# Feature sums queued behind the delta-rule branch's last evacuation, and accumulating transfers regrouped, in a hybrid transformer block

## The chip, the core and the metric

The kernel runs on one core of a Trainium2 chip. The metric is the device time of one execution in microseconds. A run of a kernel gives the median of several executions; one execution more is taken with the hardware profiler, and all rows shown come from that one.

## What is computed

One block on a sequence of 512 tokens with 1024 features. A projection `w_in` feeds two branches: A, a gated delta rule with 8 heads, and B, retention with 4 heads. Both are gated, added, projected and normed; a feed-forward part with 4096 hidden features follows.

```python
xn = rmsnorm(x, n_mix_pre)
proj = xn @ w_in
qa, ka, va, za, beta_logit, a_dt, qb, kb, vb, gb, gate_a, gate_b = _split_cols(proj, IN_SIZES)
...
oa = chunk_gated_delta_rule(qa, ka, va, beta, g)
oa = rmsnorm(oa, norm_a) * jax.nn.silu(za.reshape(b, s, A_HEADS, A_DV))
ya = oa.reshape(b, s, A_V) @ w_br_a
...
ob = chunk_retention(qb, kb, vb)
ob = rmsnorm(ob, norm_b.reshape(B_HEADS, B_DV)) * jax.nn.silu(gb.reshape(b, s, B_HEADS, B_DV))
yb = ob.reshape(b, s, B_V) @ w_br_b
mix = (jax.nn.sigmoid(gate_a) * ya + jax.nn.sigmoid(gate_b) * yb) @ w_out
x = x + rmsnorm(mix, n_mix_post)
hn = rmsnorm(x, n_mlp_pre)
ff = jnp.square(jax.nn.relu(hn @ w_up)) @ w_down
return x + rmsnorm(ff, n_mlp_post)
```

## The kernel before

**Matmuls.** Every large product is done in three matmuls (`mm3`, L79): both operands are split in a high and a low part, and high x high, high x low and low x high are added in PSUM. `weights` (L86) loads 512 KB of weights from DRAM into a tile `raw` (a DMA on SP), ACT casts it to `whi` (L109) and DVE subtracts to get `wlo` (L110). There are two `raw` buffers and three of `whi` and `wlo`; so SP issues a load when the `wlo` two loads earlier is done, and ACT casts when PE has finished the load three earlier. One load feeds 24 matmuls of 128x512. Products gather in four PSUM banks `mm`; scores and small products use three banks `dl`.

**Branch A.** Its heads go in four pairs `g2`. Each has `recurrence` (a chain of small matmuls with casts `vn` on ACT between them), `values_queries` of the next pair, `gated`, and `ya_partial`, which multiplies the gated rows `og` of a pair by `w_br_a`, in two halves, and adds the four banks of each half into `acc` on DVE (L443). The last, `ya_partial(3, prev)`, runs in head 0 of branch B.

**Branch B.** Each of its four heads computes `scores(h)`: q and k products, `rotary` on DVE (tiles `ro`, then `qr` and `kr` as high and low parts), then the score matmuls `dl<-qr,kr`, masked on DVE with the tile `dec` (one buffer, filled by a POOL DMA). Head 0 then has `ya_partial(3)` and the product for gate A (its four banks are emptied by a `tanh` on ACT, `g_t`, L927); the other heads multiply the head before by `w_br_b`. Last in each head is `outputs`: values and gates, scores times values (`dl<-vr,s`, emptied by DVE's `o` and ACT's `osq`), norm and gating, and transposes of `o`.

Values and gates are computed with fewer products, Strassen-Winograd style, on 2x2 blocks. That needs sums of blocks of the weights and of the activations. The weight sums of head h, `vg_sums[h]`, are made in DRAM: plain copies on SP, trickled behind weight loads, then eight transfers on POOL that add 512 KB each into a copy (L134). They form chains, in the order (2,0), (1,0), (3,0), (2,2), (1,2), (3,2), (0,0), (0,2) of block and part: block 1 adds block 2, block 3 adds block 1; the rest add from `w_in`. They are read by head h's `raw<-sums` loads. The activation sums are `feature_sums` (L745): eight additions into `full` and four pairs of a cast on ACT and a subtraction on DVE into `xsum`, each on 128x1024; they are first read in head 0's `outputs`.

**What sets the order.** The program is written without engine queues; a scheduler sorts the instructions of each engine by priority (written order, with raised priority for weights) and each engine then runs its list strictly in that order. `tc.issue_after(ins)` puts the instructions of a block behind `ins` on its engine; `keep_in_program_order` keeps them in written order. The groups of additions are hung on POOL instructions: a marker of branch A (`pool_marks`) and the `decay` DMA of a head.

Of the kernel before, what the change touches and what calls it, by code (L numbers as in the profile page):

```python
# [15 lines left out]
ALU = mybir.AluOpType  # L16
# [44 lines left out]
def hybrid_block_kernel(ctx: ExitStack, tc: tile.TileContext, a: dict, out: bass.AP):  # L61
    nc = tc.nc
# [53 lines left out]
    class BlockSums:  # L116
# [10 lines left out]
        def copy(self, i, k):  # L127
            nc.sync.dma_start(self.t[i][:, k : k + 2, :], self.first[i][:, k : k + 2, :])

        def add(self):  # L130

            for i, k in ((2, 0), (1, 0), (3, 0), (2, 2), (1, 2), (3, 2), (0, 0), (0, 2)):
                src = (self.w12, self.t[2], self.w12, self.t[1])[i]
                add = nc.gpsimd.dma_start(self.t[i][:, k : k + 2, :], src[:, k : k + 2, :], accum_op=ALU.add)  # L134
                tc.keep_in_program_order(add)

        def weights(self, i, ks):
            return block_weights(self.t[i - 1][:, 2 * ks : 2 * ks + 2, :])
# [235 lines left out]
    def gated_features(o_t, norms):  # L374
        og = [act.tile([P, 4, T], F32R, tag="og", name="og") for _ in range(2)]
        for f in range(4):
            ps = psx.tile([P, 4, P], F32, tag="tr", name="tr", bufs=1)
            for t in range(4):
                transpose(ps[:, t, :], o_t.feature(t, f))
            split_from(ps.rearrange("p t c -> p (t c)"), og[0][:, f, :], og[1][:, f, :], norms(f))  # L380
        return og

    def branch_partial(w, og, krow0):
        for half in range(2):
            yield half, feature_major(w, og, half * 512, 512, 4, krow0)
# [50 lines left out]
    def ya_partial(g2, og):  # L436
        for half, pss in branch_partial(w_br[0], og, 4 * g2):
            for f in range(4):
                dst = acc[:, half * 4 + f, :]
                if g2 == 0:  # L440
                    nc.scalar.copy(dst, pss[f])
                else:
                    nc.vector.tensor_tensor(dst, dst, pss[f], ALU.add)  # L443

    with tc.tile_pool(name="pa", bufs=1) as pa:
        kf = pa.tile([P, 8, T], F32, name="kf")
# [81 lines left out]
        pool_marks = []  # L528
# [167 lines left out]
        def gated(g2, rows, pool):  # L696
            pss = token_major(w_in, x_tile, OFF_ZA + g2 * 512, 8)
            zz = pool.tile([P, 4, T], F32, tag="zz", name="zz")
            gate_rows(pss, rows, lambda t: zz[:, t, :])

        vg_sums = [BlockSums(w_in, OFF_VB + h * 512, OFF_GB + h * 512, f"vg{h}") for h in range(4)]
        with tc.tile_pool(name="pa2", bufs=1) as pa2:
            keys(0, pa2)
            scr = base_inverse(0, pa2)
            vq = values_queries(0, pa2)
            keys(1, pa2)
            double_blocks(pa2, scr, 0)
            og = None
            for g2 in range(4):
                rows = recurrence(g2, vq, pa2)  # L710
                if g2 == 0:
                    double_blocks(pa2, scr, 8)
                    scr = base_inverse(1, pa2)
                if g2 < 3:
                    vq = values_queries(g2 + 1, pa2)
                if g2 == 1:
                    double_blocks(pa2, scr, 16)
                    double_blocks(pa2, scr, 24)
                if g2 in (1, 2):
                    with tc.issue_after(pool_marks[-1].ins):  # L720
                        vg_sums[g2 - 1].add()
                gated(g2, rows, pa2)
                if g2:
                    ya_partial(g2 - 1, og)
                og = gated_features(rows, lambda f: na[:, f % 2 : f % 2 + 1])
        prev = og


    with tc.tile_pool(name="pb", bufs=1) as pb_:
# [6 lines left out]
        def tmp(name):  # L736
            return pb_.tile([P, T], F32, tag="tm", name=name, bufs=8)


        def quarter(kh, th):  # L740
            return [x[:, 4 * kh : 4 * kh + 4, 256 * th : 256 * th + 256] for x in xs]
# [3 lines left out]
        def feature_sums():  # L745
            full = [pb_.tile([P, 2, 4, 256], F32, tag=f"vr{i}", name="full") for i in range(2)]
            a11, a12, a21, a22 = full[0][:, 0], full[0][:, 1], full[1][:, 0], full[1][:, 1]
            for a, (kh, th) in ((a21, (0, 1)), (a22, (1, 1)), (a11, (0, 0)), (a12, (1, 0))):
                h, l = quarter(kh, th)
                nc.vector.tensor_tensor(a, h, l, ALU.add)  # L750
            nc.vector.tensor_tensor(a22, a21, a22, ALU.subtract)
            nc.vector.tensor_tensor(a21, a11, a21, ALU.subtract)
            nc.vector.tensor_tensor(a11, a22, a11, ALU.subtract)
            nc.vector.tensor_tensor(a12, a12, a11, ALU.add)
            for i, a in enumerate((a22, a11, a21, a12)):
                s = pb_.tile([P, 2, 4, 256], F32R, tag=f"xs{i}", name="xsum")
                nc.scalar.copy(s[:, 0], a)
                nc.vector.tensor_tensor(s[:, 1], a, s[:, 0], ALU.subtract)
                quarters[f"s{i + 1}"] = [s[:, 0], s[:, 1]]
# [83 lines left out]
        def scores(h):  # L843
            dec = pb_.tile([P, T], F32, tag="dec", name="dec")
            decay = nc.gpsimd.dma_start(dec, a["c_decay"][h])
            if h in (1, 2):
                with tc.issue_after(decay.ins):
                    vg_sums[h + 1].add()
            qs, ks = (pb_.tile([P, 2, 2, T], F32R, tag=nm, name=nm) for nm in ("qr", "kr"))
            qs, ks = [qs[:, 0], qs[:, 1]], [ks[:, 0], ks[:, 1]]  # L850
            rotary(feature_major(w_in, xs, OFF_QB + h * 256, 256, 8), qs)
            rotary(feature_major(w_in, xs, OFF_KB + h * 256, 256, 8), ks)
            scs = []
            for i in range(4):
                t0 = min(i * P, 256)
                n = T - t0
                ps = psx.tile([P, T], F32, tag="dl", name="dl", bufs=3)
                for kk in range(2):
                    mm3(
                        ps[:, :n],  # L860
                        [ks[j][:, kk, i * P : (i + 1) * P] for j in range(2)],
                        [qs[j][:, kk, t0:T] for j in range(2)],
                        kk == 0,
                        kk == 1,
                    )
                n2 = T - i * P
                sc = tmp("sc")
                nc.vector.tensor_tensor(sc[:, :n2], ps[:, n - n2 : n], dec[:, :n2], ALU.mult)
                sh, sl = (pb_.tile([P, n2], F32R, tag=f"s{i}{j}", name="s") for j in range(2))
                nc.scalar.copy(sh, sc[:, :n2])  # L870
                nc.vector.tensor_tensor(sl, sc[:, :n2], sh, ALU.subtract)
                scs.append((sh, sl))
            return scs
# [44 lines left out]
        for h in range(4):  # L918
            scs = scores(h)
            if h == 0:  # L920
                feature_sums()
                ya_partial(3, prev)
                for half in range(2):
                    pss = gate_product(OFF_GA, half)
                    for f in range(4):
                        ta = tmp("g_t")
                        nc.scalar.activation(ta, pss[f], AF.Tanh, scale=0.5)  # L927
                        dst = acc[:, half * 4 + f, :]
                        nc.vector.scalar_tensor_tensor(dst, ta, 1.0, dst, ALU.add, ALU.mult)
                    nc.gpsimd.dma_start(ya_d[:, half * 4 : half * 4 + 4, :], acc[:, half * 4 : half * 4 + 4, :])  # L930
            else:
                for half, pss in branch_partial(w_br[1], prev, 4 * (h - 1)):
                    for f in range(4):
                        dst = accb[:, half * 4 + f, :]
                        if h == 1:
                            nc.scalar.copy(dst, pss[f])
                        else:
                            nc.vector.tensor_tensor(dst, dst, pss[f], ALU.add)
            if h == 0:
                raw_pools.append((pb_, "ych"))  # L940
            rows = outputs(h, scs)
            prev = gated_features(rows, lambda f: nb[:, 4 * h + f : 4 * h + f + 1])
# [6 lines left out]
        for half in range(2):  # L949
            pss = gate_product(OFF_GBR, half)  # L950
# [22 lines left out]
    with tc.tile_pool(name="pm", bufs=1) as pm:  # L973
# [113 lines left out]
        for grp in range(4):  # L1087
# [8 lines left out]
            for half in range(2):  # L1096
                c0 = grp * 1024 + half * 512
                for tt in [slice(0, 256), slice(256, 512)] if grp + half == 0 else [slice(0, T)]:
                    pss = feature_major(w_up, [h[:, :, tt] for h in hn], c0, 512, 8)
# [6 lines left out]
            if grp < 3:  # L1106
                for half in range(2):
                    pss = token_major(w_down, ff_tile, half * 512, 8, grp * 8)
                    for t in range(4):
                        dst = facc[:, t, half * 512 : half * 512 + 512]  # L1110
# [4 lines left out]
            else:  # L1115
                wk = og_keeps() + ff_keeps()
                for i in range(2):
                    h = pm.tile([P, 8, T], F32R, tag=f"hn{i}", name="keep").rearrange("p k t -> p (k t)")
# [39 lines left out]
```

## Time and profile before

| | us |
|---|---|
| median of 3 runs | 1403.16 |
| lowest and highest | 1402.61 and 1406.29 |
| the profiled execution | 1403.7 |
| its span, first to last instruction | 1402.0 |

| stage, from the span's start | us |
|---|---|
| the two groups of added transfers in branch A | 287.8 to 329.3 and 394.2 to 432.2 |
| head 0: feature sums on DVE | 499.0 to 533.1 |
| head 0: first product that reads them | 601.9 |
| groups behind the `dec` of heads 1 and 2 | 528.8 to 562.1 and 670.2 to 709.4 |

A row of a timeline has the start in us, the duration in us, engine, line, operation, tiles (written <- read), shape and count, and in square brackets how long the engine stood idle before and for what. A row of the waits has the waiting engine and instruction, what it waited for, us in total, times, and the longest. A row of a table of stretches has the stretch, its length, busy us (and instructions) of PE, PEld, DVE, ACT and POOL, the granted PE clock as a share, the share of the DMA engines' time and GB/s. A row of DMA issues has the tiles, the queue, the count, the size and the median us from issue to landing.

### The profile page before, as it was taken

How to read it: one execution, taken by the hardware profiler on the slowest of the kernel's cores; microseconds unless marked ns; L12 is line 12 of the kernel's file. 1: busy time of each engine (PE TensorE's matmuls, PEld its weight loads, DVE VectorE, ACT ScalarE, POOL GpSimd, SP SyncE). 2: the span in 40 equal slices, each digit the busy share in tenths (PEclk: the TensorE clock that was granted, in tenths of full speed). 3: DMA queues.
4: the chain of work that ended last, by engine and by line, in shares of the span. 5: the costliest groups of instructions: out<-in, count | busy, mean ns of one | idle time of the engine just before them, and what ended most of it. 6: DMA issues, size and time to landing. Idle time of an engine off the chain costs nothing.

```text
span 1402.0 us, 17608 instructions
## 1 busy us (share of the span) xinstructions
PE 1373.8 (98%) x6670; PEld 1125.1 (80%) x6670; DVE 869.2 (62%) x1539; ACT 613.4 (44%) x1134; POOL 86.4 (6%) x136
## 2 busy tenths in 40 slices
PE   8999999999999998999999999999999999999997
PEld 6888787787888877887878878878788888888886
DVE  5599889853765584367467576575685334344445
ACT  6778564725534241353543343443454333232331
POOL 1112300211011002000100000000000000000000
PEclk9999999999999999999999999999999999999999
DMA  5244624377365337672782442541724322323321
GB/s 158 76 136 139 191 76 151 116 159 205 104 130 115 103 128 158 175 220 83 176 224 61 142 138 89 187 143 62 252 80 134 100 95 95 101 91 104 105 76 61
DMA packets 88311, 180.08 MB, mean 128 GB/s; under 512 B 6079, under 2 KB 19537, under 8 KB 87714
## 3 DMA queue, kind: packets, MB, share of 16 engines
q1 hardware_dynamic: 77264, 148.39, 33.6%
q0 software_dynamic: 10240, 29.32, 10.5%
q8 instruction: 52, 0.85, 0.2%
q10 hardware_dynamic: 722, 1.25, 0.2%
q14 instruction: 33, 0.27, 0.1%
HBM read 173.17 MB, written 39.32 MB: 152 GB/s over the span
## 4 chain that ended last, share of the span: by engine, by line
PE 55%; DVE 3%; DMA 2%; ACT 1%; issue 1%; DVEq 0%; ACTq 0%; SPq 0%
PE mm L82 14%; PE mm L84 14%; PE mm L83 14%; PE mm L772 9%; PE dl L772 1%; PE dl L82 1%; PE dl L84 1%; PE dl L83 1%; DMA raw<-in_w_in_dram 1%; PE tr L219 1%; DMA raw<-in_w_out_dram 1%; DVE wlo L110 1%; ACT whi L109 0%; DVE tb L966 0%; DVE actT L968 0%
## 5 line engine op out<-in xcount | busy, mean ns | idle before, releaser
L110 DVE TENSOR_TENSOR wlo<-raw,whi 128x1024 fp32r<-128x1024 f32 x232 | 283.4, 1222 | 349.6 <-ACT whi L109 348.5
L109 ACT CAST whi<-raw 128x1024 fp32r<-128x1024 f32 x232 | 243.9, 1052 | 467.9 <-PE mm L83 257.0
L84 PE MATMUL mm<-actT,wlo 128*128 128x512 f32 (+1 forms) x528 | 208.8, 396 | 0.0
L83 PE MATMUL mm<-actT,whi 128*128 128x512 f32 (+1 forms) x528 | 207.4, 393 | 1.2 <-DVE actT L253 1.2
L82 PE MATMUL mm<-actT,whi 128*128 128x512 f32 (+1 forms) x528 | 207.0, 393 | 0.8 <-ACT actT L252 0.8
L82 PEld LDWEIGHTS mm<-actT,whi 128*128 128x128 f32 x528 | 100.0, 190 | 20.9 <-ACT actT L252 1.2
L83 PEld LDWEIGHTS mm<-actT,whi 128*128 128x128 f32 x528 | 100.0, 189 | 20.6 <-DVE actT L253 1.4
L84 PEld LDWEIGHTS mm<-actT,wlo 128*128 128x128 f32 x528 | 100.2, 190 | 18.8
L82 PE MATMUL mm<-hn,whi 128*128 128x512 f32 (+1 forms) x288 | 105.6, 367 | 0.6 <-DVE r L1081 0.5
L82 PE MATMUL mm<-og,whi 128*128 128x512 f32 x256 | 101.1, 395 | 4.6 <-DVE acc L443 4.4
L83 PE MATMUL mm<-hn,whi 128*128 128x512 f32 (+1 forms) x288 | 105.3, 366 | 0.0
L84 PE MATMUL mm<-hn,wlo 128*128 128x512 f32 (+1 forms) x288 | 105.1, 366 | 0.0
L83 PE MATMUL mm<-og,whi 128*128 128x512 f32 x256 | 100.7, 393 | 0.0
L84 PE MATMUL mm<-og,wlo 128*128 128x512 f32 x256 | 100.6, 393 | 0.0
L82 PE MATMUL mm<-whi,actT 128*128 128x512 f32 x216 | 86.2, 399 | 0.0
L83 PE MATMUL mm<-wlo,actT 128*128 128x512 f32 x216 | 85.9, 398 | 0.0
L84 PE MATMUL mm<-whi,actT 128*128 128x512 f32 x216 | 85.6, 397 | 0.0
L772 PE MATMUL mm<-whi,xsum 128*128 128x512 f32 x256 | 80.2, 390 | 0.0
L407 DVE SCALAR_TENSOR_TENSOR c_y<-c_raw,convw,c_y 128x512 f32<-128x512 f32 x96 | 70.5, 751 | 3.4 <-ACT c_y L405 2.8
L82 PEld LDWEIGHTS mm<-hn,whi 128*128 128x128 f32 x288 | 54.3, 188 | 10.2 <-DVE r L1081 0.8
L84 PEld LDWEIGHTS mm<-hn,wlo 128*128 128x128 f32 x288 | 54.2, 189 | 8.8
L83 PEld LDWEIGHTS mm<-hn,whi 128*128 128x128 f32 x288 | 54.3, 188 | 8.6
(319 smaller groups left out, 2463.8 us busy)
## 6 DMA issues: line engine op xcount, KB each, us to landing
raw<-in_w_in_dram SPq DMA_DIRECT2D x105, 512.0 KB, 3.8
raw<-in_w_up_dram SPq DMA_DIRECT2D x36, 512.0 KB, 3.8
sums<-in_w_in_dram SPq DMA_DIRECT2D x32, 512.0 KB, 5.2
raw<-sums SPq DMA_DIRECT2D x32, 512.0 KB, 4.4
raw<-in_w_down_dram SPq DMA_DIRECT2D x32, 512.0 KB, 3.7
raw<-in_w_br_a_dram SPq DMA_DIRECT2D x16, 512.0 KB, 3.9
sums<-in_w_in_dram POOLq DMA_DIRECT2D x16, 512.0 KB, 11.6
sums<-sums POOLq DMA_DIRECT2D x16, 512.0 KB, 7.5
```

The source lines that it names most:

```text
L82: nc.tensor.matmul(ps, lh, rh, start=first, stop=False)
L83: nc.tensor.matmul(ps, lh, rl, start=False, stop=False)
L84: nc.tensor.matmul(ps, ll, rh, start=False, stop=last)
L109: nc.scalar.copy(hi[:, :n], raw[:, :n])
L110: nc.vector.tensor_tensor(lo[:, :n], raw[:, :n], hi[:, :n], ALU.subtract)
L219: nc.tensor.transpose(ps, src, ident)
L407: nc.vector.scalar_tensor_tensor(y, raw[:, j : j + T], tap(j), y, ALU.mult, ALU.add)
L772: m = nc.tensor.matmul(pss[t], lhs[i // 2], rhs[i % 2], start=first and k + i == 0, stop=k + i == 5, skip_group_check=not first,)
```

## The change

Two things are changed. The feature sums of head 0 are written after `ya_partial(3)` and put behind its last `acc` addition on DVE. And the 32 accumulating transfers, unchanged in themselves and in their order, form one sequence from which groups are drawn: 10 and 12 at the two places in branch A and 8 and 2 behind the `dec` of heads 1 and 2, where before each place issued the eight of one head. The lines of the changed kernel are shifted by up to 7; the order on SP stays as it was.

```diff
-        def add(self):
+        def adds(self):
             for i, k in ((2, 0), (1, 0), (3, 0), (2, 2), (1, 2), (3, 2), (0, 0), (0, 2)):
                 src = (self.w12, self.t[2], self.w12, self.t[1])[i]
-                add = nc.gpsimd.dma_start(self.t[i][:, k : k + 2, :], src[:, k : k + 2, :], accum_op=ALU.add)
-                tc.keep_in_program_order(add)
+                yield self.t[i][:, k : k + 2, :], src[:, k : k + 2, :]
...
-                    nc.vector.tensor_tensor(dst, dst, pss[f], ALU.add)
+                    added = nc.vector.tensor_tensor(dst, dst, pss[f], ALU.add)
+        return added if g2 else None
...
+        adds = itertools.chain.from_iterable(sums.adds() for sums in vg_sums)
+        def add_blocks(mark, n):
+            with tc.issue_after(mark.ins):
+                for dst, src in itertools.islice(adds, n):
+                    tc.keep_in_program_order(nc.gpsimd.dma_start(dst, src, accum_op=ALU.add))
...
                 if g2 in (1, 2):
-                    with tc.issue_after(pool_marks[-1].ins):
-                        vg_sums[g2 - 1].add()
+                    add_blocks(pool_marks[-1], 8 + 2 * g2)
...
             if h in (1, 2):
-                with tc.issue_after(decay.ins):
-                    vg_sums[h + 1].add()
+                add_blocks(decay, 8 if h == 1 else 2)
...
             if h == 0:
-                feature_sums()
-                ya_partial(3, prev)
+                with tc.issue_after(ya_partial(3, prev).ins):
+                    feature_sums()
```

On DVE, in head 0 of branch B, from the last rotary step of k to the gate product (`kr`, `sc` and `s` belong to the scores, `acc` to `ya_partial(3)`), the order before ends so:

```order
L753 TENSOR_TENSOR full<-full 128x1024
L868 TENSOR_TENSOR sc<-dl,dec 128x512
L868 TENSOR_TENSOR sc<-dl,dec 128x384
L868 TENSOR_TENSOR sc<-dl,dec 128x256
L754 TENSOR_TENSOR full<-full 128x1024
...
L758 TENSOR_TENSOR xsum<-full,xsum 128x1024 x2
L110 TENSOR_TENSOR wlo<-raw,whi 128x1024
L758 TENSOR_TENSOR xsum<-full,xsum 128x1024
L443 TENSOR_TENSOR acc<-acc,mm 128x512 x4
L110 TENSOR_TENSOR wlo<-raw,whi 128x1024
L443 TENSOR_TENSOR acc<-acc,mm 128x512 x4
```

In the changed kernel the same place reads:

```order
L442 TENSOR_TENSOR acc<-acc,mm 128x512 x4
L110 TENSOR_TENSOR wlo<-raw,whi 128x1024 x2
L442 TENSOR_TENSOR acc<-acc,mm 128x512 x4
L757 TENSOR_TENSOR full<-actT 128x1024
L110 TENSOR_TENSOR wlo<-raw,whi 128x1024
L757 TENSOR_TENSOR full<-actT 128x1024 x3
L110 TENSOR_TENSOR wlo<-raw,whi 128x1024
L758 TENSOR_TENSOR full<-full 128x1024
L759 TENSOR_TENSOR full<-full 128x1024
L765 TENSOR_TENSOR xsum<-full,xsum 128x1024
L760 TENSOR_TENSOR full<-full 128x1024
L110 TENSOR_TENSOR wlo<-raw,whi 128x1024
```

All twelve instructions of the sums, which began among the rotary steps before, now stand behind both sets of `acc` additions, among the `wlo` of the gate product.

On POOL, from the second group in branch A to the first `dec` of branch B (`at` is the marker's tile, `rope` the table that the rotary steps read), the order before is:

```order
L608 AFFINE_SELECT at<-at 128x1024
L134 DMA sums<-in_w_in_dram 128x2x512
L134 DMA sums<-sums 128x1024 x2
L134 DMA sums<-in_w_in_dram 128x2x512
L134 DMA sums<-sums 128x1024 x2
L134 DMA sums<-in_w_in_dram 128x2x512 x2
L731 DMA rope<-in_c_rope_dram 128x1024
```

And in the changed kernel:

```order
L608 AFFINE_SELECT at<-at 128x1024
L708 DMA sums<-sums 128x1024
L708 DMA sums<-in_w_in_dram 128x2x512
L708 DMA sums<-sums 128x1024 x2
L708 DMA sums<-in_w_in_dram 128x2x512 x3
L708 DMA sums<-sums 128x1024 x2
L708 DMA sums<-in_w_in_dram 128x2x512
L708 DMA sums<-sums 128x1024 x2
L738 DMA rope<-in_c_rope_dram 128x1024
```

Twelve additions stand ahead of `rope` in place of eight; three that wait for no sum stand together in the middle, after the end of one head's chain.

Further down POOL's list, from the stores of `ya_d` to its reload behind the heads, the order before is:

```order
L930 DMA ya_d<-acc 128x2048 x2
L845 DMA dec<-in_c_decay_dram 128x512
L134 DMA sums<-in_w_in_dram 128x2x512
L134 DMA sums<-sums 128x1024 x2
L134 DMA sums<-in_w_in_dram 128x2x512
L134 DMA sums<-sums 128x1024 x2
L134 DMA sums<-in_w_in_dram 128x2x512 x2
L845 DMA dec<-in_c_decay_dram 128x512
```

And in the changed kernel:

```order
L936 DMA ya_d<-acc 128x2048 x2
L852 DMA dec<-in_c_decay_dram 128x512
L708 DMA sums<-in_w_in_dram 128x2x512 x2
L852 DMA dec<-in_c_decay_dram 128x512
```

The first `dec` here is head 2's, issued while head 1 runs; two additions follow it where there were eight.

## The prediction

> **What bounds the kernel now.** The page comes first, for the engine that sets the time, then the waits of that engine over the whole run.
>
> ```profile
> PE 1373.8 (98%) x6670; PEld 1125.1 (80%) x6670; DVE 869.2 (62%) x1539; ACT 613.4 (44%) x1134; POOL 86.4 (6%) x136
> ```
>
> ```profile
> PE mm L82 <- DVE acc L443: 4.4, 1, 4.4
> PE dl L82 <- ACT osq L904: 2.2, 1, 2.2
> ...
> PE dl L82 <- ACT kr L840: 0.7, 1, 0.7
> PE dl L82 <- DVE p L824: 0.7, 1, 0.7
> ...
> PE mm L82 <- DVE ro L836: 0.2, 1, 0.2
> ```
>
> PE is busy for 1373.8 of 1402.0 us, so only its few waits, and matmuls slower than usual, can be won. The five waits shown lie at two places. Three belong to head 0 of the retention, where the change moves the feature sums; the two on `osq` and `p` belong to head 1, where it takes transfers away. PE's timeline shows what each costs:
>
> ```profile
> 516.79 0.39 PE L84 MATMUL mm<-og,wlo 128*128 128x512 f32 x1
> 517.38 0.50 PE L82 MATMUL mm<-og,whi 128*128 128x512 f32 x1 [0.20 <-DVE ro L836]
> 518.62 0.50 PE L82 MATMUL dl<-qr,kr 128*128 128x512 f32 x1 [0.75 <-ACT kr L840]
> ...
> 528.78 0.39 PE L83 MATMUL mm<-og,whi 128*128 128x512 f32 x1
> 529.01 0.39 PE L84 MATMUL mm<-og,wlo 128*128 128x512 f32 x1
> 533.80 0.79 PE L82 MATMUL mm<-og,whi 128*128 128x512 f32 x1 [4.40 <-DVE acc L443]
> ...
> 539.79 0.39 PE L84 MATMUL mm<-og,wlo 128*128 128x512 f32 x1
> ```
>
> Starts of undisturbed 128x512 matmuls are 0.23 us apart (528.78 to 529.01). Every start-to-start above that is loss. DVE's timeline at the same place says why PE stood still:
>
> ```profile
> 528.52 2.35 DVE L758 TENSOR_TENSOR xsum<-full,xsum 128x1024 fp32r<-128x1024 f32 x2
> ...
> 531.93 1.22 DVE L758 TENSOR_TENSOR xsum<-full,xsum 128x1024 fp32r<-128x1024 f32 x1
> 533.07 2.47 DVE L443 TENSOR_TENSOR acc<-acc,mm 128x512 f32<-128x512 f32 x4
> ```
>
> All four `mm` banks were full at 529.2, and the `acc` additions that empty them stood behind the feature sums in DVE's queue until 533.07.
>
> **Term 1, the queue on DVE.** (a) The wait at the bank: 533.80 - 529.01 - 0.23 = **4.6 us**. In the new order the four additions stand ahead of all twelve feature-sum instructions, and each can run as its bank fills; the first bank is complete some 18 matmuls (4.1 us) before PE asks for it. (b) The half-speed stretch behind the wait:
>
> ```profile
> 533.80:539.80 6.00, 6.00 (x15) 4.69 (x16) 1.74 (x3) 0.00 (x0) 0.86 (x1) 0.52 0.75 169
> ```
>
> The granted clock is 0.52 there, and 14 starts take 539.79 - 533.80 = 5.99 in place of 14 x 0.227 = 3.18: **2.8 us**, which goes with the wait. (c) Ahead of the scores PE loses 517.38 - 516.79 - 0.23 = 0.36 and 518.62 - 517.38 - 0.23 = 1.01, since sums of 1.2 us each stand between the rotary steps on DVE. The four heads run the same rotary, and each of these two waits occurs once in the whole run, in the head with the sums. So of 0 to 1.4 I take **1.2**, near the three heads that don't wait, with a little left as PE's order around the scores changes too.
>
> Where the sums go, and what they hide behind:
>
> ```profile
> L772 PE MATMUL mm<-whi,xsum x256: 388/389/499, 601.9 to 919.2; 128*128 128x512 f32 x128
> ```
>
> ```profile
> 547.50:569.30 21.80, 21.80 (x98) 18.03 (x97) 7.42 (x8) 6.01 (x7) 4.01 (x4) 1.00 0.90 192
> ```
>
> Twelve instructions of the 1.22 us that the row at 531.93 shows, which overlap by some 0.07, are some 14 us. They now fall beside the first half of the gate product (547.5 to 569.3 before), where DVE has 21.80 - 7.42 = 14.4 us free, and spill a few us at most. Their first reader is at 601.9, over 30 us later. Queued behind them are the `wlo` of the gate product's weights:
>
> ```profile
> 547.54 1.05 ACT L109 CAST whi<-raw 128x1024 fp32r<-128x1024 f32 x1 [4.39 <-PE mm L83]
> ```
>
> This cast waits for PE to free a ring slot and is two loads, 2 x 5.44 us, ahead of use, so a `wlo` may be 8 us late. The `tanh` casts on ACT that empty the gate banks stand behind `xsum` casts (1.05 us each) and `whi` casts; following both queues in the new order I find the fourth bank free some 2 us before PE asks. Its cost is 0 if weight loads land in about 8 us, and up to 4 if they take the longest found below; I take 0, as loads beside one add at a time come near the short end.
>
> **Term 2, head 1.** The group of eight transfers that ran in head 1 becomes two:
>
> ```profile
> 670.22 1.23 POOL L134 DMA_DIRECT2D sums<-in_w_in_dram  x1
> ...
> 706.75 2.63 POOL L134 DMA_DIRECT2D sums<-in_w_in_dram  x2
> ```
>
> ```profile
> 718.98 1.05 ACT L109 CAST whi<-raw 128x1024 fp32r<-128x1024 f32 x1 [4.22 <-DMA raw<-in_w_in_dram]
> ...
> 722.96 1.05 ACT L109 CAST whi<-raw 128x1024 fp32r<-128x1024 f32 x1 [1.88 <-DMA raw<-in_w_in_dram]
> ```
>
> ```profile
> raw<-in_w_in_dram SPq DMA_DIRECT2D x6, 512.0 KB, 9.6
> raw<-in_w_in_dram SPq DMA_DIRECT2D x5, 512.0 KB, 3.8
> ```
>
> The first of the last two rows is the loads issued from 705 to 722 us, the second those from 800 to 817, the same stretch of head 2, which has no adds: 9.6 us against 3.8. The late loads hold ACT's queue, and with it the scores' output:
>
> ```profile
> 724.83 0.39 PE L84 MATMUL dl<-vr,s 128*128 128x512 f32 x1
> 725.91 0.50 PE L82 MATMUL dl<-vr,s 128*128 128x512 f32 x1 [0.69 <-DVE p L824]
> ...
> 730.58 0.39 PE L84 MATMUL mm<-actT,wlo 128*128 128x512 f32 x1
> 733.16 0.50 PE L82 MATMUL dl<-vr,s 128*128 128x512 f32 x1 [2.20 <-ACT osq L904]
> ...
> 737.60 0.40 PE L82 MATMUL mm<-actT,whi 128*128 128x512 f32 x1
> ```
>
> 0.85 + 2.35, and 12 starts in 4.44 in place of 2.72, 1.72 of half speed: **4.9 us**. As a check, the first transpose of `o` comes in each head:
>
> ```profile
> 642.50 0.33 PE L219 MATMUL tr<-cmat,o 128*128 128x128 f32 x1 [0.41 <-DVE o L910]
> 742.70 0.34 PE L219 MATMUL tr<-cmat,o 128*128 128x128 f32 x1 [0.34 <-DVE o L910]
> 837.76 0.33 PE L219 MATMUL tr<-cmat,o 128*128 128x128 f32 x1 [0.41 <-DVE o L910]
> ```
>
> Head 1 takes 100.2 and head 2 95.1, 5.1 more for the same matmuls. The two adds left run in the first 15 us of the stretch, far from 705.
>
> The half-speed part can be weighed against a rule. The Trainium skill, "TensorE: Matmul & The Clock Gate", section "What's actually happening", has the clock fall only after an idle window of about 3.4 us; the 4.40 us wait fits. The wait at 733 is 2.20 us, and the clock still fell; by the rule the 1.72 would not belong to it and the term would be 3.2. The trace shows the fall, so 4.9 stays.
>
> **Term 3, what the moved transfers hit.** Six more adds now run from 394 on (12 for 8), so four stand together at about 414 to 419 where before the last three came at 429:
>
> ```profile
> 394.20 1.17 POOL L134 DMA_DIRECT2D sums<-in_w_in_dram  x1
> ...
> 429.53 2.65 POOL L134 DMA_DIRECT2D sums<-in_w_in_dram  x2
> 498.12 0.62 POOL L731 DMA_DIRECT2D rope<-in_c_rope_dram  x1 [65.94 <-PE tr L219]
> ```
>
> ```profile
> 428.23 1.05 ACT L109 CAST whi<-raw 128x1024 fp32r<-128x1024 f32 x1 [4.38 <-PE mm L83]
> ```
>
> The weights of this cast leave SP some 8.5 us ahead of it, now amid the four, and behind the cast stands the recurrence's `vn`. The nearest case is the first group, whose adds met the same stage:
>
> ```profile
> 328.32 1.05 ACT L109 CAST whi<-raw 128x1024 fp32r<-128x1024 f32 x1 [1.47 <-DMA raw<-in_w_in_dram]
> ```
>
> ```profile
> 330.86 0.70 PE L650 MATMUL dl<-vn,kd 128*128 128x256 f32 x2 [0.81 <-ACT vn L645]
> ```
>
> 1.47 us late cost PE 0.8. The bounds are 0 and head 1's 4.9; I take **0.8 lost**, the nearest row. The two adds more in the first group fall into 329 to 355, where only one weight load is issued, with over 10 us to spare: 0.
>
> The Trainium skill, "DMA: Bandwidth & Descriptors", section "Queues, rings and completion order", says each DMA engine takes turns between queue rows packet by packet. By it, adds waiting in one row would hinder a load no more than a single add, which speaks against any worth in regrouping; it is the first rival.
>
> `rope`, `dec` and `ya_d` are moved behind more adds on POOL. The five dependent links from 394.20 to 429.00 took 7 us each; six links and the issues end near 460, and `rope` waits for its buffer until 498.12, as before: 38 us of cover. `ya_d` and the later `dec` have as much room as before. SP issues in the same order.
>
> **Sum.** 4.6 + 2.8 + 1.2 + 4.9 - 0.8 = 12.7 us off the profiled execution's 1403.7 gives 1391.0; that execution is 0.5 above the median of 1403.16, so **1390.5** is forecast.
>
> **Rivals.**
> - *The lateness moves with the adds.* Whatever is taken from head 1 is paid where the adds now run, up to head 1's 4.9 again in place of 0.8: 1394.6. For it: the same bytes move, and loads beside adds are 9.6 against 3.8 us. Against: the loads near 420 have 8.5 us, and the recurrence after them issues hardly any.
> - *ACT's chain in the gate product.* Three adds now start together near 523; weights issued at 525 and 530 may be late, and `xsum` casts that wait for DVE then hold back the `tanh` that empties the banks. A wait of 2 to 4 us with a half-speed stretch of 2.8: 1396.3. Against: the worked-out queue leaves 2 us.
> - *Slower: `rope` late.* If the twelve adds ran beyond 498, rotary would start late, and after some 8 us of slack each us is PE's. It is slower than before once the adds end after about 519 (498 + 8 + 12.7); 20 us past the slack give 1410.5. That needs links of some 19 us; those seen are 7, so it is unlikely.
> - *It doesn't do what it says.* The compiled order shows the additions ahead of the sums, so only an unforeseen wait could give 1403.
>
> **How the numbers follow.** Chances: forecast (1388 to 1393) 0.68, lateness moves 0.17, gate chain 0.08, no effect 0.04, slower 0.03. The range takes the first two and half of the third: 1388.0 to 1397.0. A measurement of this kernel can tell about 0.3% (4.2 us) from no change. The first three cases are all below 1399: faster 0.92 with a little off for their far ends, 0.91; within 0.3% 0.05; slower 0.04.
>
> **What would show it.** Right: no PE wait on `acc`, none on `osq`, granted clock 1.00 behind both places, heads 1 and 2 equal to 0.5 us, loads of head 1 near 4 us. Wrong: a PE wait on `vn` above 2 us near 430, one on `g_t` in the gate product, or `rope` issued after 500.

## The result

Six executions of each kernel give 1403.89 us before (1400.48 to 1406.29) and **1392.11 us after** (1390.61 to 1394.03): a ratio of 0.9917, with a 95% interval of 0.9901 to 0.9932. Forecast were 1390.5, between 1388.0 and 1397.0. The profiled execution of the changed kernel is 1392.33 us, against 1403.7 before: 11.4 us less, where the sum had 12.7.

The page of the changed kernel, its row of engines, and then what is left on lines of head 0, head 1 and the stage of the moved transfers among the waits of PE:

```profile
PE 1368.6 (98%) x6670; PEld 1123.1 (81%) x6670; DVE 870.1 (63%) x1539; ACT 614.0 (44%) x1134; POOL 86.3 (6%) x136
```

```profile
PE tr L218 <- DVE o L916: 1.7, 4, 0.4
...
PE dl L650 <- ACT vn L645: 1.5, 2, 1.0
...
PE mm L82 <- DVE zz L369: 0.6, 1, 0.6
```

The waits on `acc`, `osq`, `kr`, `p` and `ro` are not in the list any more. The one on `o`, 0.4 in each head, was there before too; `vn` and `zz` are the places that the first ten and twelve transfers touch. The table of stretches over the places of the two waits that brought half speed before, and PE's timeline where it had stood still ahead of the scores:

```profile
528.00:540.00 12.00, 12.00 (x54) 9.95 (x53) 4.41 (x6) 2.11 (x2) 0.13 (x1) 1.00 0.98 210
725.00:740.00 15.00, 14.58 (x71) 11.53 (x69) 11.83 (x27) 4.07 (x6) 0.00 (x0) 1.00 0.14 38
```

```profile
518.61 0.39 PE L84 MATMUL mm<-og,wlo 128*128 128x512 f32 x1
518.84 0.39 PE L82 MATMUL dl<-qr,kr 128*128 128x512 f32 x1
```

PE is busy for all of the first stretch, and the granted clock is 1.00 in both, where 0.52 stood behind `acc`. The scores' first matmul starts 0.23 us after the product ahead of it, which is the undisturbed distance.

**Where the time went.** ACT's casts of weights are the same instructions in both kernels and mark the same places of the program. Three of them, before and after, lie behind the moved transfers in branch A, behind head 0's gate product, and behind the late loads of head 1. The first one of before, at 428.23, is in the prediction.

```profile
574.70 1.05 ACT L109 CAST whi<-raw 128x1024 fp32r<-128x1024 f32 x1 [2.46 <-PE mm L83]
...
741.72 1.05 ACT L109 CAST whi<-raw 128x1024 fp32r<-128x1024 f32 x1 [2.44 <-PE mm L83]
```

```profile
430.01 1.05 ACT L109 CAST whi<-raw 128x1024 fp32r<-128x1024 f32 x1 [4.91 <-DMA raw<-in_w_in_dram]
...
567.70 1.05 ACT L109 CAST whi<-raw 128x1024 fp32r<-128x1024 f32 x1 [3.90 <-PE mm L83]
...
729.49 1.05 ACT L109 CAST whi<-raw 128x1024 fp32r<-128x1024 f32 x1 [2.38 <-PE mm L83]
```

The changed kernel is 1.78 us late at the first, 7.00 early at the second and 12.23 early at the third. So head 0 gave 8.8 us, head 1 gave 5.2, and 1.8 had been lost before. From there to the last cast on this line (1350.70 and 1339.29) 0.8 goes back. Most of it, 0.7, goes between the casts of 994.33 and 1036.26 (982.21 and 1024.82 after), a stretch that nothing moved; the same stretch took between 0.9 us less and 0.7 more than before in the profiles of the other runs.

The first transpose of `o` in each head, after:

```profile
635.44 0.33 PE L218 MATMUL tr<-cmat,o 128*128 128x128 f32 x1 [0.41 <-DVE o L916]
730.55 0.33 PE L218 MATMUL tr<-cmat,o 128*128 128x128 f32 x1 [0.42 <-DVE o L916]
825.64 0.33 PE L218 MATMUL tr<-cmat,o 128*128 128x128 f32 x1 [0.41 <-DVE o L916]
```

Heads 1 and 2 take 95.11 and 95.09 us, where 100.20 and 95.06 stood. The DMA issues of head 1 from 695 to 712 us, the stretch whose loads took 9.6 us before:

```profile
raw<-in_w_in_dram SPq DMA_DIRECT2D x6, 512.0 KB, 3.7
```

And the price, in the timelines of POOL, ACT and PE where the twelve transfers run:

```profile
414.57 3.80 POOL L708 DMA_DIRECT2D sums<-in_w_in_dram  x3
```

```profile
424.04 1.05 ACT L109 CAST whi<-raw 128x1024 fp32r<-128x1024 f32 x1 [5.05 <-DMA raw<-in_w_in_dram]
```

```profile
432.06 1.13 PE L650 MATMUL dl<-vn,kd 128*128 128x256 f32 x4 [1.05 <-ACT vn L645]
```

The three issues of 414.57 come right behind a fourth at 414.03. The casts of 424.04 and 430.01 now wait for their load, where those of before waited for PE, and PE waits 1.05 us for `vn`.

### The profile page after: what moved, and what is told of

Its sections match the earlier page's. It is cut to its first block, busy times and chain, and to the rows that moved or that the text cites. A ratio compares the mean times of both kernels' runs of the same rounds, so it can differ in the third digit from the quotient of the medians.

```text
span 1390.6 us, 17607 instructions
## 1 busy us (share of the span) xinstructions
PE 1368.6 (98%) x6670; PEld 1123.1 (81%) x6670; DVE 870.1 (63%) x1539; ACT 614.0 (44%) x1134; POOL 86.3 (6%) x136
## 3 DMA queue, kind: packets, MB, share of 16 engines
q10 hardware_dynamic: 722, 1.25, 0.2%
## 4 chain that ended last, share of the span: by engine, by line
PE 87%; DVE 6%; DMA 4%; ACT 2%; issue 1%; SPq 0%; DVEq 0%; ACTq 0%
PE mm L84 21%; PE mm L83 21%; PE mm L82 21%; PE mm L779 9%; PE tr L218 2%; DMA raw<-in_w_in_dram 2%; PE dl L779 2%; DVE wlo L110 1%; PE dl L84 1%; PE dl L82 1%; PE dl L83 1%; PE dl L670 1%; DVE c_y L406 1%; PE dl L642 1%; ACT whi L109 1%
```

## The experiments

Every kernel was timed beside the one before; a line gives the median, the span of its executions, and the ratio with its 95% interval.

| run | us | lowest to highest | ratio to before |
|---|---|---|---|
| e1_queue_only | 1394.46 | 1393.94 to 1396.25 | 0.9936 (0.9921 to 0.9951) |
| e2_groups_only | 1401.58 | 1397.41 to 1403.58 | 0.9985 (0.9973 to 0.9998) |
| e3_pairs | 1395.42 | 1394.25 to 1399.34 | 0.9945 (0.9926 to 0.9965) |
| e4_six_in_head1 | 1392.11 | 1389.92 to 1393.51 | 0.9916 (0.9897 to 0.9935) |
| e5_written_after | 1392.64 | 1390.42 to 1393.41 | 0.9924 (0.9899 to 0.9949) |
| e6_two_subs_behind | 1393.41 | 1392.40 to 1394.09 | 0.9932 (0.9908 to 0.9955) |
| e7_one_sub_behind | 1397.42 | 1396.49 to 1401.16 | 0.9964 (0.9950 to 0.9979) |
| e8_ten_in_head0 | 1389.00 | 1387.83 to 1391.56 | 0.9903 (0.9878 to 0.9928) |
| e9_changed_again | 1391.29 | 1389.91 to 1393.21 | 0.9920 (0.9905 to 0.9936) |
| e10_ten_again | 1389.55 | 1388.58 to 1391.63 | 0.9911 (0.9896 to 0.9926) |

The theory is that of the prediction: head 0 gains since `acc` no longer stands behind the sums on DVE, head 1 gains since its loads meet no transfers, and the moved transfers cost a little where they now run.

### Each half alone

Only the new place of the sums, in the kernel before:

```diff
-                    nc.vector.tensor_tensor(dst, dst, pss[f], ALU.add)
+                    added = nc.vector.tensor_tensor(dst, dst, pss[f], ALU.add)
+        return added if g2 else None
...
-                feature_sums()
-                ya_partial(3, prev)
+                with tc.issue_after(ya_partial(3, prev).ins):
+                    feature_sums()
```

> Only the feature sums are moved behind the last acc addition; the transfers stay in groups of 8, 8, 8 and 8. My theory: the two terms are independent, so this wins 8.6 us (4.6 wait on acc, 2.8 half speed, 1.2 before the scores) and nothing in head 1: 1395.2 against a kernel before of 1403.9. Head 1 stays 5 us longer than head 2, with the waits on p and osq. Rival: the waits of the two heads hang together through the transfers in flight (adds beside head 0's loads), so that one part alone wins clearly less than 8 or clearly more than 9.

It won 9.1 us (1403.56 to 1394.46), where the casts give head 0 8.8 in the changed kernel, and 8.4 in this kernel's own profile. That is neither clearly less than 8 nor clearly more than 9, so nothing speaks for the rival. Head 1 kept its waits:

```profile
PE dl L82 <- ACT osq L905: 2.2, 1, 2.2
...
PE dl L82 <- DVE p L825: 1.5, 1, 1.5
```

Only the new groups, with the sums as before:

```diff
-                with tc.issue_after(ya_partial(3, prev).ins):
-                    feature_sums()
+                feature_sums()
+                ya_partial(3, prev)
```

> Only the groups of 10, 12, 8 and 2; the feature sums stand where they stood. My theory: 5.0 us won in head 1, 0.8 to 2 lost near 402 and 430 where four adds run together: 3 to 4 won, 1400.3. PE's wait of 4.4 us on acc and the half-speed stretch behind it stay. Rival: the transfers at the front of the group in head 0 also change the wait on acc, by over 1 us.

It won 2.0, less than expected, and the two halves together make 11.1 of the 11.8 that the medians of the whole change show. Head 1 takes 95.05 us here, so its 5.1 are fully there. In the profile the rest is lost in head 0, ahead of the wait on `acc`. This profile is the slowest of ten executions (1403.58, where the median is 1401.58), so the loss that it shows is likely above the usual one. PE's timeline, the stretch of the scores, and DVE's first rotary step:

```profile
520.64 0.49 PE L82 MATMUL mm<-og,whi 128*128 128x512 f32 x1 [1.49 <-DVE ro L843]
521.89 0.50 PE L82 MATMUL dl<-qr,kr 128*128 128x512 f32 x1 [0.75 <-ACT kr L847]
...
538.44 0.80 PE L82 MATMUL mm<-og,whi 128*128 128x512 f32 x1 [4.19 <-DVE acc L442]
```

```profile
520.00:525.00 5.00, 3.60 (x12) 2.83 (x13) 5.00 (x7) 2.27 (x3) 0.00 (x0) 0.82 0.36 110
```

```profile
506.49 0.69 DVE L840 TENSOR_TENSOR ro<-mm,rope 128x512 f32<-128x512 f32 x1 [3.17 <-DMA rope<-in_c_rope_dram]
```

The wait on `ro` was 0.20 before and is 1.49, and the clock falls behind it. DVE's first rotary step waited for `rope`, and with the sums between the rotary steps nothing makes up for it. This is (c) of term 1, which the prediction put at 1.2; the next experiments measure it apart.

### How many sums may stand ahead of `acc`

The sums written behind `ya_partial(3)`, but not hung behind its last addition. The scheduler then leaves the first eight sums among the rotary steps and puts the four `xsum` subtractions behind the first four `acc` additions:

```diff
-                with tc.issue_after(ya_partial(3, prev).ins):
-                    feature_sums()
+                ya_partial(3, prev)
+                feature_sums()
```

> The changed kernel, with the feature sums written after ya_partial(3) but not put behind its last addition. In the compiled order DVE then has the first four acc additions ahead of the four last sums, but the first eight sums stay among the rotary and score steps, as before. So this takes away (a) and (b) of term 1 and leaves (c). Theory (the wait on acc is where the queue cost): no PE wait on acc, and only (c) is missing against the changed kernel, 1.2 us by the forecast, up to 3 if rope lands as late as in the run with the groups alone, where PE waited 1.49 us on ro and 0.75 on kr at a clock of 0.83. That gives 1393.3 to 1395.5, 1394.2 as one number. Rival (all twelve sums have to stand behind): a wait on acc of 4 us comes back and the time is 1399 or more.

No wait on `acc` is left, and the time, 1392.64, is 1.6 below the expectation and among the executions of the changed kernel. The rival (all twelve must stand behind) falls. PE's timeline has the two waits of (c):

```profile
516.77 0.50 PE L82 MATMUL mm<-og,whi 128*128 128x512 f32 x1 [0.80 <-DVE ro L843]
518.02 0.50 PE L82 MATMUL dl<-qr,kr 128*128 128x512 f32 x1 [0.75 <-ACT kr L847]
```

This profile is 3.0 us ahead of that of the changed kernel at the cast before the scores (511.74 against 514.77) and 1.0 ahead behind them (528.62 against 529.62), so (c) costs 2.0 here. The medians alone, 0.5 apart, don't show it.

Next, two of the four subtractions into `xsum` stand behind `acc` and the rest ahead of it, as before; then only one behind. The second kernel differs from the first in the two numbers (3 in place of 2):

```diff
+            split = []
...
-                nc.vector.tensor_tensor(s[:, 1], a, s[:, 0], ALU.subtract)
+                split.append((s, a))
...
+            subtract(split[:2])
+            return lambda: subtract(split[2:])
...
+                rest = feature_sums()
                 with tc.issue_after(ya_partial(3, prev).ins):
-                    feature_sums()
+                    rest()
```

> The changed kernel, with only the last two of the four subtractions into xsum behind the acc additions and everything else of the sums ahead of them, written as before. The first addition then stands behind one sum of 1.2 us less than three: in the rows of before it would start at 529.7 in place of 533.07, and the wait on acc would be 1.0 us in place of 4.4. Theory: (c) is lost as in the run that is written after without the constraint (1.2 to 3 us), the wait of 1.0 comes on top, and the clock stays at 1.00 behind it, since waits of 1.05, 1.41 and 1.44 us in the looks so far left it at 1.00 and those of 2.20 and 2.62 did not: 1394.3 to 1396.5, 1395.2 as one number. Rival (any wait at that place halves the clock): 2.8 us more, 1398.

> The changed kernel, with only the last of the four subtractions into xsum behind the acc additions. By the rows of before the first addition would start at 531.9 in place of 533.07: a wait on acc of 3.3 us, and with it a half-speed stretch of some 2.5. Theory: 1.2 to 3 us for (c), 3.3 and 2.5: 1399.1 to 1401, 1399.6 as one number. Rival (the clock falls only after an idle time of about 3.4 us): the clock behind the wait is 1.00 and the time is 1396.6 to 1398.4.

PE's timeline and the stretch of 6 us at the place, first with two behind, then with one:

```profile
532.41 0.50 PE L82 MATMUL mm<-og,whi 128*128 128x512 f32 x1 [1.01 <-DVE acc L442]
```

```profile
528.00:534.00 6.00, 4.99 (x23) 3.81 (x22) 6.00 (x10) 1.66 (x3) 4.11 (x4) 1.00 0.75 154
```

```profile
533.01 0.79 PE L82 MATMUL mm<-og,whi 128*128 128x512 f32 x1 [3.28 <-DVE acc L442]
...
538.72 0.41 PE L83 MATMUL mm<-og,whi 128*128 128x512 f32 x1
```

```profile
534.00:540.00 6.00, 6.00 (x18) 4.70 (x17) 0.75 (x2) 0.00 (x0) 0.00 (x0) 0.61 1.10 236
```

The waits are 1.01 and 3.28 us, as worked out from the queue (1.0 and 3.3). Behind the first the clock stays at 1.00. Behind the second it falls, and 13 starts take 5.71 us in place of 2.95: 2.8 more. So one subtraction (1.2 us of DVE) and one `wlo` in the wrong place make 2.3 us of wait and 2.8 of half speed; between the medians lie 4.0 of these 5.1. All three kernels of this part are 1.6 to 2.2 us below what was expected; the kernel before, timed beside them, was itself 1.1 lower (1402.80 against 1403.89). The last one's 1397.42 even lies in its rival's range, so the times don't decide between them; the clock does. In both, the rival falls by it: a wait of 1.01 didn't halve the clock, and one of 3.28, under 3.4, did.

How large (c) is hangs on when `rope` lands. In the five profiles that have the sums among the rotary steps, the time from its issue on POOL to the first rotary step on DVE, beside the wait on `ro`:

| profile | issue to first step, us | PE's wait on `ro`, us |
|---|---|---|
| e7_one_sub_behind | 503.57 - 498.55 = 5.0 | under 0.2 |
| before | 503.23 - 498.12 = 5.1 | 0.20 |
| e5_written_after | 502.62 - 496.87 = 5.8 | 0.80 |
| e6_two_subs_behind | 505.24 - 499.32 = 5.9 | 0.97 |
| e2_groups_only | 506.49 - 500.08 = 6.4 | 1.49 |

Each tenth of a microsecond past 5.0 is PE's. In the seven profiles with all sums behind, it took 5.3 (the changed kernel and e3), 5.7 (e4), 6.0 (e8), 6.1 (e10), 6.2 (the second profile of the changed kernel, e9) and 6.7 (e1), and PE didn't wait for `ro` in any. How much room is left shows in DVE's rotary steps for k in the changed kernel, and in PE's timeline of e1:

```profile
514.96 0.69 DVE L842 TENSOR_TENSOR ro<-mm,rope 128x512 f32<-128x512 f32 x1 [0.87 <-PE mm L84]
```

```profile
517.20 0.50 PE L82 MATMUL dl<-qr,kr 128*128 128x512 f32 x1 [0.17 <-ACT kr L841]
```

At 5.3 DVE still waits 0.87 us for PE, and at 6.7 PE waits for `kr`; between the casts around the scores e1 takes 0.5 us more than the changed kernel. So without the sums `rope` may take about 6.2 us at no cost, some 1.2 more than with them.

### Amount or place of the transfers

Six transfers in head 1 in place of two, taken from the twelve:

```diff
-                    add_blocks(pool_marks[-1], 8 + 2 * g2)
+                    add_blocks(pool_marks[-1], 12 - 2 * g2)
...
-                add_blocks(decay, 8 if h == 1 else 2)
+                add_blocks(decay, 8 if h == 1 else 6)
```

> The changed kernel with groups of 10, 8, 8 and 6, so six adds run in head 1. My theory: only loads from 705 us on (8 us earlier here, 697) have too little room, and six adds, whose chain is shorter, land before about 700; head 1 costs at most 1.5 us more than head 2 and the time is 1392 to 1393.5. Rival: each add in head 1 costs its share of 5.1 us, so six cost 0.64 x 6 = 3.8, of which two were there: 2.6 more, 1394.7 or above.

1392.11, the median of the changed kernel. The first transposes of `o` in heads 0 and 1:

```profile
635.02 0.33 PE L218 MATMUL tr<-cmat,o 128*128 128x128 f32 x1 [0.41 <-DVE o L916]
730.31 0.33 PE L218 MATMUL tr<-cmat,o 128*128 128x128 f32 x1 [0.41 <-DVE o L916]
```

Head 1 takes 95.29 us, 0.2 over head 2 of the changed kernel. POOL's timeline has the last issue of the six:

```profile
682.05 2.62 POOL L708 DMA_DIRECT2D sums<-in_w_in_dram  x2
```

The last two of the six landed 15.5 us after their issue, near 698, and the loads of `w_in` issued from there to 715 took 3.8 us. The loads of `sums` issued beside them, from 686 to 697, took 8.9 us where the changed kernel has 4.2 (from 688 to 712), and PE waited for none of them. The eight of before were issued until 706.75, beside the loads of 705 to 722. So six transfers that end before those loads cost head 1 next to nothing, and eight that run beside them cost it 5 us. The rival (each transfer has its price) falls. Eight transfers that end early were not run, so number and place are not told apart further than that.

In branch A, too, this kernel has eight transfers in its second group, as before, but they still start two places later in the sequence, so four are issued together at 414, as in the changed kernel. PE's wait on `vn` is 0.89 there. So it isn't the number that brings this wait.

The other order of the transfers, so that the three from `w_in` don't stand together:

```diff
-            for i, k in ((2, 0), (1, 0), (3, 0), (2, 2), (1, 2), (3, 2), (0, 0), (0, 2)):
+            for i, k in ((2, 0), (1, 0), (0, 0), (3, 0), (2, 2), (1, 2), (0, 2), (3, 2)):
```

> The changed kernel with the eight adds of a head in another order, so that an add that waits for none stands behind each that waits: (2,0), (1,0), (0,0), (3,0), (2,2), (1,2), (0,2), (3,2). Never more than two or three are in flight. My theory: it is the bunch of four at 414 to 419 that makes the casts near 424 and 430 late (by 1.3 and 1.8 us) and PE wait on vn; without it these casts are in time within 0.5 us, the wait on vn is below 0.4, and the time is 1 to 1.5 us less than the changed kernel's: 1390.8. Rival: it is the number of bytes moved beside the loads, however bunched: the same lateness and 1392.

A miss: 3.3 us above the changed kernel. The late load only comes elsewhere. In the first group two transfers at a time now run beside the loads of 303 to 328 us; ACT, PE and the stretch behind the wait:

```profile
330.11 1.04 ACT L109 CAST whi<-raw 128x1024 fp32r<-128x1024 f32 x1 [3.29 <-DMA raw<-in_w_in_dram]
```

```profile
332.64 0.70 PE L650 MATMUL dl<-vn,kd 128*128 128x256 f32 x2 [2.62 <-ACT vn L645]
```

```profile
333.00:340.00 7.00, 7.00 (x30) 5.66 (x29) 3.74 (x7) 2.61 (x7) 0.00 (x0) 0.76 1.05 181
```

2.62 us of wait and a clock of 0.76 behind it; by 351 us the run is 3.6 us behind the changed kernel. In the changed kernel the three issued together at 327 met only loads whose casts come over 20 us later. Near 430 the theory held, with no PE wait on `vn`, but a wait of 1.27 on `zz` at 415 came in its place, and from 401 to 451 this kernel loses 1.6 us, about as much as the kernels with the bunch.

Groups of 8, 8, 10 and 6: branch A as before, nothing late in head 1:

```diff
-                    add_blocks(pool_marks[-1], 8 + 2 * g2)
+                    add_blocks(pool_marks[-1], 8)
...
-                add_blocks(decay, 8 if h == 1 else 2)
+                add_blocks(decay, 10 if h == 1 else 6)
```

> The changed kernel with groups of 8, 8, 10 and 6 in place of 10, 12, 8 and 2: branch A has the groups of before, with no bunch of three or more at 414 us; head 0 takes two adds more, and head 1 six, which the run with six there showed to be free. Theory (a loss hangs on where adds meet weight loads that are about to be used): the waits on zz at 411 and on vn at 432 and the late casts between go, head 1 stays at the length of head 2: 2 us less than the changed kernel, 1390.1. Rivals: the two adds more in head 0 delay loads of the gate product or of head 0's outputs: 1392 to 1394; or the lateness between 400 and 432 is that of any group there and stays: 1392.1.

1389.00, the fastest of all; head 1 takes 95.08 us. It was run again beside the changed kernel on one chip:

> The changed kernel as it stands, timed beside the one with groups of 8, 8, 10 and 6 on the same chip, since so far each was only compared with before. 1392.1 by its own runs; its waits on zz and vn between 400 and 432 and the late casts there come back in this look, if they are the kernel's and not one run's.

> The groups of 8, 8, 10 and 6 again, beside the changed kernel on the same chip. Theory (the lateness between 400 and 432 is that of the moved adds): no wait there of over 0.3 us, and 2 to 3 us less than the changed kernel: 1389.5. Rival (both have the same time, and the two differ by their runs): 1392.

1389.55 against 1391.29: 1.7 us less, where 2 to 3 were expected, with executions that overlap (1388.58 to 1391.63 and 1389.91 to 1393.21), so the two are likely but not surely apart in time. PE's rows near 430 us, in the changed kernel and in this one:

```profile
432.73 1.13 PE L650 MATMUL dl<-vn,kd 128*128 128x256 f32 x4 [1.10 <-ACT vn L645]
```

```profile
429.70 1.13 PE L650 MATMUL dl<-vn,kd 128*128 128x256 f32 x4 [0.43 <-ACT vn L645]
```

The wait on `vn` came back in the changed kernel, the one on `zz` did not. With the other groups a wait of 0.43 is left, a little over the 0.3 that was expected at most. Over all profiles the wait on `vn` near 430 is a matter of the groups. In the seven with 10 transfers first, in the change's order (the changed kernel twice, e2, e4, e5, e6, e7), it is 1.05, 1.10, 1.41, 0.89, 1.05, 0.67 and 0.39 us, 0.9 on average; in the four with 8 and 8 (before, e1, e8, e10) it is 0 three times and 0.43 once. The wait on `zz` near 411 came in three of the seven (0.61, 0.63, 0.88) and in none of the four. Between the casts of 401.26 and 451.45 of before, the seven take 0.7 to 2.5 us more than before, 1.6 on average, and the other three of the four 0 to 0.6 more.

The groups of 8 aren't free of late loads: in e1, e8 and e10 the cast that stands at 417.35 before waited 7.4 to 7.6 us for its load. No `vn` stands close behind that one, and it cost nothing that PE's waits show.

## Why the prediction was right

- **Term 1 (a), the wait at the bank, 4.6: right.** Without the sums ahead of `acc` it is gone; with two, one or none of the last subtractions behind `acc` it is 1.01, 3.28, and 4.19 to 4.40 us, as DVE's queue gives.
- **Term 1 (b), half speed, 2.8: right.** It comes and goes with the wait: clock 0.61 behind 3.28 us, 1.00 behind 1.01.
- **Term 1 (c), ahead of the scores, 1.2: right in its place, not a constant.** By the casts on both sides of the scores it was 1.4 in the profile that the forecast read, and 1.3 to 4.3 in the others with the sums there (the largest, e2, with a fall of the clock). It is the wait on `kr`, and what `rope` takes to land past 5.0 us; that profile was one with a short landing, which was luck. In the changed kernel it is nil.
- Together 8.6 were forecast. From 428.23 to 580.14 of before, six of the seven profiles with all sums behind gain 8.7 to 8.9 by the casts, and e1, with the late `rope`, 8.4.
- **What the sums hide behind: right.** No PE wait on `g_t`, on `wlo` or on `xsum`, even in e1, where a cast at 569.52, in the gate product, waited 7.22 us for its load. The rival in the gate product is out.
- **Term 2, head 1, 4.9: right.** 5.1 by the transposes, loads at 3.7 us. Its cause, transfers beside loads about to be used, is told apart from a price for each transfer by the six that cost nothing.
- **Term 3, 0.8 lost near 428: right in the mechanism, too small.** The wait on `vn` was 1.05 in the first profile and 0.9 on average. The wait on `zz`, 0.3 on average, was missing from the term: the second group now begins with a chained transfer and a free one side by side at 394, and the cast of 408.07 waited 2.45 us for its load. By the casts the stretch lost 1.6 on average, and 0.2 with groups of 8: 1.4 for the moved transfers. That the bunch as such is the cause isn't shown. The number of transfers isn't it (with eight in that group, in e4, the wait stayed), but pairs in place of the bunch lost as much, by `zz`. In the profiles here a late load cost PE something where a step that PE waits for (`vn`, `zz`) stood behind its cast.
- **The rival that the lateness moves with the transfers** falls: of the 5.1 that head 1 gave, 1.4 is paid elsewhere, and with groups of 8, 8, 10 and 6 nearly nothing.
- **`rope` late:** its buffer sets its issue, as forecast, and so it moves with what PE lost before: 1.78 us later than before in the first profile (499.90), 2.45 in the second (500.57, past the 500 that was named as a sign of being wrong, and harmless). The 8 us of slack behind it that this rival counts on aren't there; about 1.2 are.
- **Slips of the working that changed nothing:** four more transfers run from 394 on, not six (12 for 8; the other two are in the first group), and the first three chances add up to 0.93, not 0.92.

In the first profile the sum was 1.3 us too large (12.7 forecast, 11.4 measured). Terms 1 and 2 gave 14.0, 0.5 more than forecast. The stage of term 3, between the casts of 401.26 and 428.23, lost 2.1 where 0.8 were forecast. The rest is scatter that no step of the sum names, and here it came to 0.5 lost: 1.0 stands already at the cast of 27.25 (28.20 after), ahead of everything that the change touches, with a granted clock between 10 and 20 us of 0.87 before and 0.50 after; 1.3 come back between the casts of 245.93 and 351.51, 0.8 of them where the wait on `vn` of before near 331 didn't occur; and 0.8 went after head 1. That the total lies this close is in part luck.

## What to carry to other kernels

When matmuls fill every bank, ask which instruction empties the next one and what is queued ahead of it on its engine; work with a late reader goes behind it, and even one stray instruction of 1.2 us, and the one that it keeps ahead, can turn a harmless wait into a fall of the clock. What bulk transfers cost depends on the loads beside them: here they cost time beside loads with a chain close behind them, and six or ten ran for nothing where the loads beside them had room. Work put between two steps that wait for a transfer also uses up the slack for that transfer's late landing, which one profile may not show.

## What the runs showed of the hardware

**How long a wait brings the clock down.** In busy stretches, single PE waits of 1.01, 1.05, 1.41, 1.44, 1.46 and 1.89 us left the granted clock at 1.00; those of 2.16, 2.20, 2.62, 3.28 and 4.40 brought it down. The longest that did not, from the second profile of the changed kernel, with the stretch behind it, and then the shortest that did, from the kernel with the sums alone:

```profile
331.78 0.70 PE L650 MATMUL dl<-vn,kd 128*128 128x256 f32 x2 [1.89 <-ACT vn L645]
```

```profile
332.00:335.00 3.00, 3.00 (x16) 2.31 (x16) 1.81 (x4) 0.78 (x2) 0.00 (x0) 1.00 1.07 189
```

```profile
725.23 0.50 PE L82 MATMUL dl<-vr,s 128*128 128x512 f32 x1 [2.16 <-ACT osq L905]
```

```profile
725.00:730.00 5.00, 4.77 (x14) 3.80 (x15) 1.57 (x3) 1.55 (x6) 0.00 (x0) 0.66 0.08 31
```

Two waits close together may act as one: 1.49 and 0.75 within 1.25 us, 2.24 in all, came with a clock of 0.82 in the kernel with the groups alone; 0.97 and 0.74, 1.71 in all, left it at 1.00. Between 10 and 20 us of the run, where several waits of 1 to 2 us follow each other, the size of one wait doesn't decide: behind one of 1.24 us at 16 us the clock was 0.72 in the kernel before and 1.00 in e5. The Trainium skill, "TensorE: Matmul & The Clock Gate", section "What's actually happening", puts the fall behind an idle window of about 3.4 us. Here a wait of 2.16 was enough, so the measurement decides.

**The same transfers, other luck.** The wait on `vn` near 331 us, behind eight transfers that are alike in all kernels but e3, was 0 to 1.89 us over eleven profiles. A term of a microsecond that hangs on a load's landing needs several profiles.
